# Weight splits pinned to the written order, and transposes of the compressed keys further behind their rotation

## The chip, the cores and the metric

The kernel runs on one core of one Trainium2 chip. The metric is the device time of one execution in microseconds (us), the median of several runs. The engines are named as the profile names them: PE multiplies matrices (PEld loads its weights), DVE is the vector engine, ACT the scalar engine, POOL the general one, SP the queue that issues the loads. Each engine has its own instruction stream and works through it in order; an instruction that waits for another engine holds up everything behind it on its own engine.

## The reference

Two layers, 256 positions, model width 1024, all in float32. What matters is the shape of the work:

```
for layer in range(2):
    h = rmsnorm(x, pre_norm[layer])
    proj = h @ w_in[layer]                  # 1024 x 7704, thirteen pieces
    hq, hf, hi, hz, nq, kc, vc, ks, vs, kw, vw, ng, nz = split(proj)
    o_h = rmsnorm(hgrn2(hq, hf, hi)) * silu(hz)            # gated linear recurrence, 8 heads
    k_cmp = rope(compress(kc));  v_cmp = compress(vc)      # 15 compressed blocks
    o_n = attention(rope(nq), (k_cmp, v_cmp), (rope(ks), vs), (rope(kw), vw), ng) * silu(nz)
    y = concatenate([o_h, o_n]) @ w_out[layer]
    x = x + rmsnorm(y, post_norm[layer])
```

## The kernel before

Every weight is used once for the 256 positions. To multiply at float32 accuracy, a weight and an activation are each cut in two float32r parts, and a product is three matmuls: high by high, and the two mixed ones. The weights of both layers are 168 **units** (`plan`, L182 to L192), numbered here from 0, of 128 partitions by 1024 (or 1072) elements, 84 to a layer. A unit goes through four steps. A load of 512 KB on SP's queue brings it into one of five `raw` buffers. ACT copies it to `whi`, rounded to the high part (L202). DVE subtracts that from `raw` and writes the rest to `wlo` (L203). Then PE uses both, in six to 24 matmuls; `whi` and `wlo` have eight buffers each.

The projections are written in the order nq, hf (here called the forget gates), kc/vc, kw, ks, hq, hi, hz, nz and then the output projection. PE's lines: L368 to L370 (`mm_a`: activations moving, 128x512 or narrower), L378 to L380 (`mm_b`: 128x256), L492/L493 (the compression), L997 to L999 (output projection). L351 transposes the normalised `h` of each half `a` of the positions, ACT's L355 and DVE's L356 make `Hhi` and `Hlo` of it, and these are what the next layer's first matmuls wait for.

What else DVE and ACT do beside the splits, as far as it is named below:
- The recurrence (`hgrn_fast`, L767 to L814): per layer two chains of some 25 DVE instructions, with two scans each (L769, L793) of the 128x1024 elements. The first chain works in the buffers `sA0` to `sA3`, the second in `sB0` to `sB3`.
- `kcvc` (L477 on ACT, L478 on DVE): splits the inputs of the compression into `sN0` and `sN1`; each second L477 is issued only after the first L478.
- `vals` and the gates: L560 (ACT), L561 (DVE), L587 (ACT).
- `compress`: `yp` is copied on ACT (L499), summed (L504, L506) and multiplied again (`second`); the keys are rotated (`rope`, L386 on ACT and L390 to L393 on DVE, into `kst`), transposed on PE (L531, in `third`) and split (`split_k`, L540 on ACT, L541 on DVE). The full keys take L552 for the transposes. L608 to L610 are the attention scores, which read them.
- `finish` (L1002): the end of a layer for one half `a`: L1008 and L1009, L331/L332 (root and reciprocal), L1014, then `norm_in`: L339, L344, and `turn_h` with L351.

Code is written in the order of a clock that the kernel keeps itself: each matmul advances `clock` by its ideal duration (`tick`), and `later(lag, fn, ch)` puts a function off by `lag` us of that clock. A unit's split is put off in this way by `LAG` = 9 us behind the point where its load is written, or until it is taken. That is the written order. The framework then orders each engine's stream at build time by its own estimates, so what runs may stand far from where it was written. `tc.keep_in_program_order` excludes an instruction from that: it is not issued before what was written ahead of it on its engine. Other instructions may still move.

Of the kernel before, what the change touches and what calls it, by code (L numbers as in the profile page):

```python
# [10 lines left out]
F32 = mybir.dt.float32  # L11
# [4 lines left out]
OP = mybir.AluOpType  # L16
# [25 lines left out]
CP = (2.0, 3.0)  # L42
L1 = (3.0, 3.0)
L2 = (5.0, 5.0)
L3 = 3.0
LQ = 4.0
LK = 8.0
LH = 10.0
# [47 lines left out]
def build(ctx, tc, A, out):  # L96
    nc = tc.nc
    V, S, P = nc.vector, nc.scalar, nc.tensor
# [23 lines left out]
    def later(lag, fn, ch):  # L122
        heapq.heappush(heap, (clock[0] + lag, count[0], ch, fn))
        count[0] += 1
# [69 lines left out]
    class Ring:  # L194
# [4 lines left out]
        def convert(self, n):  # L199
            while len(self.split) < n:  # L200
                raw, hi, lo, shaped = self.made[len(self.split)]
                S.copy(out=hi, in_=raw)  # L202
                V.tensor_tensor(out=lo, in0=raw, in1=hi.bitcast(F32), op=OP.subtract)  # L203
                self.split.append((shaped(hi), shaped(lo)))

        def fill(self, n=RING):
# [280 lines left out]
    def compress(l, i, ring, KC):  # L487
# [26 lines left out]
        def second():  # L514
# [19 lines left out]

            later(L3, third, "c0")

# [601 lines left out]
```

## Time and profile before

| what | value |
|---|---|
| median of 3 runs | 566.41 us (566.41 to 568.52) |
| the profiled execution | 566.25 us, its span 564.5 us |
| PE busy | 548.2 us (97% of the span) |
| PE's weight loads busy | 490.3 us (87%) |
| DVE busy | 398.0 us (71%) |
| ACT busy | 332.2 us (59%) |
| loads and stores | 96.55 MB, mean 171 GB/s |

The profile is one execution. The first two lines are times of the device; the span is the part of the execution in which engines work, and the 1.75 us beside it lie around it. Busy shares are averages over the span.

### The profile page before, as it was taken

The numbers are of one execution on the slowest core, as the hardware profiler recorded it, in microseconds if no ns is written. First come the engines' busy times: TensorE is split into PE (matmuls) and PEld (weight loads), VectorE is DVE, ScalarE is ACT, GpSimd is POOL, SyncE is SP. The second block draws the span as 40 slices with busy tenths as digits, with TensorE's granted clock in tenths as the row PEclk, the third lists the DMA queues.
The fourth block names the chain that finished last, engine by engine and source line by source line (L and its number), as shares of the span: only waits on it lengthen the run. The fifth ranks groups of instructions, "written<-read, shape, count | busy, mean of one in ns | idle before, by whom it ended". The sixth has DMA issues, their size and how long they took to land. (4 is left out here: it accounts for less than half of the span.)

```text
span 564.5 us, 9581 instructions
## 1 busy us (share of the span) xinstructions
PE 548.2 (97%) x3563; PEld 490.3 (87%) x3563; DVE 398.0 (71%) x880; ACT 332.2 (59%) x626; POOL 9.6 (2%) x18
## 2 busy tenths in 40 slices
PE   7999999999999999999989999999999999999993
PEld 4889998999888989988878999879988898998882
DVE  4897997889577277663678599878967654866422
ACT  6577447855366785552557763686626768746310
POOL 4000000000000001001000000000000000000000
PEclk9999999999999999999999999999999999999997
DMA  8697559953146058565475755698423622856111
GB/s 302 204 315 236 150 149 280 302 175 114 38 126 194 21 186 291 162 214 151 133 240 170 230 151 157 197 303 257 117 72 82 170 87 70 301 172 202 40 38 43
DMA packets 72196, 96.55 MB, mean 171 GB/s; under 512 B 3383, under 2 KB 49229, under 8 KB 72142
## 3 DMA queue, kind: packets, MB, share of 16 engines
q1 hardware_dynamic: 72142, 95.86, 55.3%
q8 instruction: 30, 0.49, 0.3%
q14 instruction: 24, 0.20, 0.1%
HBM read 93.75 MB, written 2.10 MB: 170 GB/s over the span
## 5 line engine op out<-in xcount | busy, mean ns | idle before, releaser
L203 DVE TENSOR_TENSOR wlo<-raw,whi 128x1024 fp32r<-128x1024 f32 (+1 forms) x168 | 202.8, 1222 | 60.4 <-ACT whi L202 57.4
L202 ACT CAST whi<-raw 128x1024 fp32r<-128x1024 f32 (+1 forms) x168 | 175.0, 1052 | 89.0 <-PE ps_mm L379 24.4
L378 PE MATMUL ps_mm<-Hhi,whi 128*128 128x256 f32 x448 | 127.5, 285 | 0.0
L379 PE MATMUL ps_mm<-Hlo,whi 128*128 128x256 f32 x448 | 125.7, 281 | 0.0
L380 PE MATMUL ps_mm<-Hhi,wlo 128*128 128x256 f32 x448 | 125.7, 280 | 0.0
L368 PE MATMUL ps_mm<-whi,Hhi 128*128 128x512 f32 (+1 forms) x256 | 101.5, 397 | 2.3 <-ACT Hhi L355 2.3
L369 PE MATMUL ps_mm<-wlo,Hhi 128*128 128x512 f32 (+1 forms) x256 | 98.9, 386 | 0.0
L370 PE MATMUL ps_mm<-whi,Hlo 128*128 128x512 f32 (+1 forms) x256 | 98.8, 387 | 0.0
L379 PEld LDWEIGHTS ps_mm<-Hlo,whi 128*128 128x128 f32 x448 | 84.5, 189 | 0.1
L378 PEld LDWEIGHTS ps_mm<-Hhi,whi 128*128 128x128 f32 x448 | 84.3, 188 | 0.1
L380 PEld LDWEIGHTS ps_mm<-Hhi,wlo 128*128 128x128 f32 x448 | 84.4, 188 | 0.0
L368 PEld LDWEIGHTS ps_mm<-whi,Hhi 128*128 128x128 f32 x256 | 48.9, 191 | 10.2 <-ACT Hhi L355 3.0
L370 PEld LDWEIGHTS ps_mm<-whi,Hlo 128*128 128x128 f32 x256 | 48.6, 190 | 10.2 <-DVE Hlo L356 0.3
L369 PEld LDWEIGHTS ps_mm<-wlo,Hhi 128*128 128x128 f32 x256 | 48.8, 191 | 7.6 <-DVE wlo L203 0.5
L627 DVE CUSTOM_DVE_ANT_0 ps_s<-ps_s,cm 128x128 f32<-128x128 f32 (+1 forms) x64 | 22.4, 370 | 2.1 <-PE ps_s L610 0.7
L630 ACT ACTIVATE sB<-ps_s,nm 128x256 f32<-128x256 f32 (+1 forms) x40 | 16.9, 430 | 10.8 <-DVE nm L627 10.1
L671 DVE TENSOR_TENSOR sB<-ps_t,sB 128x512 fp32r<-128x512 f32 x12 | 8.2, 687 | 20.1 <-ACT sB L670 20.1
L1009 DVE TENSOR_TENSOR sA<-ps_mm,sB 128x512 f32<-128x512 f32 x6 | 4.2, 692 | 21.6 <-ACT st L1008 21.6
L997 PE MATMUL ps_mm<-whi,sN 128*128 128x512 f32 x48 | 19.0, 396 | 0.0
L998 PE MATMUL ps_mm<-wlo,Hhi 128*128 128x512 f32 x48 | 19.0, 395 | 0.0
L999 PE MATMUL ps_mm<-whi,Hlo 128*128 128x512 f32 x48 | 18.9, 395 | 0.0
L999 PE MATMUL ps_mm<-whi,sN 128*128 128x512 f32 x48 | 18.9, 394 | 0.0
(282 smaller groups left out, 927.7 us busy)
## 6 DMA issues: line engine op xcount, KB each, us to landing
raw<-in_w_in SPq DMA_DIRECT2D x112, 512.0 KB, 4.6
raw<-in_w_out SPq DMA_DIRECT2D x32, 512.0 KB, 4.3
raw<-in_w_in SPq DMA_DIRECT2D x8, 536.0 KB, 4.7
raw<-in_cmp_w_k SPq DMA_DIRECT2D x16, 256.0 KB, 3.3
raw<-in_cmp_w_v SPq DMA_DIRECT2D x16, 256.0 KB, 3.3
sB<-in_x SPq DMA_DIRECT2D x3, 512.0 KB, 3.5
sB<-in_post_norm SPq DMA_DIRECT2D x2, 512.0 KB, 5.4
xs<-sB SPq DMA_DIRECT2D x4, 256.0 KB
```

The source lines that it names most:

```text
L202: S.copy(out=hi, in_=raw)
L203: V.tensor_tensor(out=lo, in0=raw, in1=hi.bitcast(F32), op=OP.subtract)
L368: P.matmul(out=ps, lhsT=hh, rhs=wh, start=k == 0, stop=False)
L369: P.matmul(out=ps, lhsT=hh, rhs=wl, start=False, stop=False)
L370: P.matmul(out=ps, lhsT=hl, rhs=wh, start=False, stop=k == KT - 1)
L378: P.matmul(out=ps, lhsT=wh, rhs=hh, start=k == 0, stop=False)
L379: P.matmul(out=ps, lhsT=wh, rhs=hl, start=False, stop=False)
L380: P.matmul(out=ps, lhsT=wl, rhs=hh, start=False, stop=k == KT - 1)
L627: V.tensor_tensor_reduce(out=sb[b], in0=sb[b], in1=mk[b], scale=-1.0, scalar=3e38, op0=OP.add, op1=OP.min, accum_out=nm[:, i, b:b + 1])
L997: P.matmul(out=ps, lhsT=hi, rhs=wh, start=first, stop=False)
L998: P.matmul(out=ps, lhsT=hi, rhs=wl, start=False, stop=False)
L999: P.matmul(out=ps, lhsT=lo, rhs=wh, start=False, stop=last)
```

## The change

Both instructions of a split, L202 on ACT and L203 on DVE, are pinned to the order in which they are written. And `L3`, the lag of `third` behind the rotation of the compressed keys, goes from 3 to 5 us of the kernel's own clock.

```diff
-L3 = 3.0
+L3 = 5.0
...
         def convert(self, n):
             while len(self.split) < n:
                 raw, hi, lo, shaped = self.made[len(self.split)]
-                S.copy(out=hi, in_=raw)
-                V.tensor_tensor(out=lo, in0=raw, in1=hi.bitcast(F32), op=OP.subtract)
+                tc.keep_in_program_order(S.copy(out=hi, in_=raw))
+                tc.keep_in_program_order(V.tensor_tensor(out=lo, in0=raw, in1=hi.bitcast(F32), op=OP.subtract))
                 self.split.append((shaped(hi), shaped(lo)))
```

The instructions are the same before and after; their order is not. Three places:

**DVE at the first layer's recurrence.** The number behind a name tells buffers apart; wlo_483, 509, 556, 574, 654, 673, 726 and 746 are the low parts of units 16 to 23. Before:

```order
71 L203 TENSOR_TENSOR wlo_509<-raw_507,whi_508 128x1024
72 L203 TENSOR_TENSOR wlo_556<-raw_554,whi_555 128x1024
73 L203 TENSOR_TENSOR wlo_574<-raw_572,whi_573 128x1024
...
99 L793 SCALAR_TENSOR_TENSOR sA3_441<-sA0_438,km_581,sN2_590 128x1023
100 L203 TENSOR_TENSOR wlo_673<-raw_671,whi_672 128x1072
101 L797 TENSOR_TENSOR sA2_440<-sA2_440,sA3_441 128x1024
102 L811 TENSOR_TENSOR sA0_438<-sA2_440,ce_579 128x512
103 L814 TENSOR_TENSOR sA0_438<-sA2_440,kx_589 128x512
104 L203 TENSOR_TENSOR wlo_726<-raw_724,whi_725 128x1072
105 L203 TENSOR_TENSOR wlo_746<-raw_744,whi_745 128x1072
106 L767 COPY fs_750<-sB0_592 128x32
```

With the change:

```order
94 L203 TENSOR_TENSOR wlo_483<-raw_481,whi_482 128x1024
95 L203 TENSOR_TENSOR wlo_509<-raw_507,whi_508 128x1024
96 L793 SCALAR_TENSOR_TENSOR sA3_441<-sA0_438,km_581,sN2_590 128x1023
97 L797 TENSOR_TENSOR sA2_440<-sA2_440,sA3_441 128x1024
98 L203 TENSOR_TENSOR wlo_556<-raw_554,whi_555 128x1024
99 L203 TENSOR_TENSOR wlo_574<-raw_572,whi_573 128x1024
100 L811 TENSOR_TENSOR sA0_438<-sA2_440,ce_579 128x512
101 L814 TENSOR_TENSOR sA0_438<-sA2_440,kx_589 128x512
102 L767 COPY fs_750<-sB0_592 128x32
103 L768 MEMSET sB0_592 128x32
104 L203 TENSOR_TENSOR wlo_654<-raw_652,whi_653 128x1072
```

The splits of units 16 to 19 stood ahead of the first chain of the recurrence and stand inside it now, and those of units 20 to 23 stood inside and ahead of the second chain and stand inside or behind it. wlo_726 and wlo_746 come after the second chain's L790.

**ACT at the compressed keys of the first layer.** Here kTh takes the high parts of the keys, whi_1200, 1212 and 1236 are units 36 to 38; ps_t_1287 before and ps_t_1340 after is the result of L531. Before, units 36 to 38 stand ahead of these rows:

```order
86 L202 CAST whi_1268<-raw_1267 128x1024
87 L202 CAST whi_1282<-raw_1281 128x1024
88 L386 ACTIVATE kst_1249<-ps_mm_1190 128x2x96
89 L540 CAST kTh_85<-ps_t_1287 128x2x15
90 L202 CAST whi_1301<-raw_1300 128x1024
91 L560 CAST vhi_90<-ps_mm_1190 128x256
92 L540 CAST kTh_85<-ps_t_1308 128x2x128
93 L499 COPY st_1323<-ps_s_1258 68x256
```

With the change:

```order
82 L386 ACTIVATE kst_1249<-ps_mm_1190 128x2x96
83 L540 CAST kTh_85<-ps_t_1303 128x2x128
84 L499 COPY st_1318<-ps_s_1258 68x256
85 L540 CAST kTh_85<-ps_t_1340 128x2x15
86 L560 CAST vhi_90<-ps_mm_1190 128x256
87 L202 CAST whi_1200<-raw_1199 128x1024
88 L202 CAST whi_1212<-raw_1211 128x1024
89 L202 CAST whi_1236<-raw_1235 128x1024
```

The copies of units 36 to 38 stood ahead of all of the keys' work and now stand behind it, behind L499 and L560 too. On PE, L531 stood in the middle of the compression's last matmuls, and now stands behind the last of them, followed at once by L608, L504 and L552, and these by unit 36.

**ACT at the boundary between the layers.** whi_3067, 3077, 3087, 3097 and 3107 are units 84 to 88, the first of the second layer; the L355 of ps_t_3125 and 3132 make `Hhi` for the first half of the positions, those of ps_t_3185 and 3192 for the second. Before:

```order
231 L202 CAST whi_3087<-raw_3086 128x1024
232 L339 ACTIVATE sA1_3050,ss_3051<-sB2_2823 128x512 x2
233 L202 CAST whi_3097<-raw_3096 128x1024
234 L202 CAST whi_3107<-raw_3106 128x1024
235 L331 ACTIVATE r1_3055<-ss_3051,eps_t_77 128x1
...
239 L355 CAST Hhi_87<-ps_t_3125 128x512
240 L355 CAST Hhi_87<-ps_t_3132 128x512
...
247 L355 CAST Hhi_87<-ps_t_3185 128x512
248 L355 CAST Hhi_87<-ps_t_3192 128x512
```

With the change:

```order
235 L202 CAST whi_3087<-raw_3086 128x1024
236 L1008 ACTIVATE st_3161,yss_3162<-ps_mm_2833 128x512
237 L1008 ACTIVATE st_3161,yss_3162<-ps_o_2834 128x512
238 L331 ACTIVATE r1_3168<-yss_3162,eps_t_77 128x1
239 L339 ACTIVATE sA3_3175,ss_3176<-sB3_2825 128x512 x2
240 L331 ACTIVATE r1_3180<-ss_3176,eps_t_77 128x1
241 L355 CAST Hhi_87<-ps_t_3185 128x512
242 L355 CAST Hhi_87<-ps_t_3192 128x512
243 L202 CAST whi_3097<-raw_3096 128x1024
244 L386 ACTIVATE st_3226<-ps_mm_3199 128x4x96
245 L202 CAST whi_3107<-raw_3106 128x1024
```

The copies of units 87 and 88 stood ahead of both halves' L355 and stand behind the second half's. On PE, the transposes of the first half (into ps_t_3125 and 3132) stood at the end of the first layer's last matmuls and now stand ahead of that layer's last nine; those of the second half stood among unit 90's matmuls, after units 84 to 89 of the first half, and now stand behind unit 86, before unit 87.

## Rows read from the trace of the kernel before

**Rows 1.** The page, busy times by engine, and the groups of the two split lines.

```profile
PE 548.2 (97%) x3563; PEld 490.3 (87%) x3563; DVE 398.0 (71%) x880; ACT 332.2 (59%) x626; POOL 9.6 (2%) x18
...
L203 DVE TENSOR_TENSOR wlo<-raw,whi 128x1024 fp32r<-128x1024 f32 (+1 forms) x168 | 202.8, 1222 | 60.4 <-ACT whi L202 57.4
L202 ACT CAST whi<-raw 128x1024 fp32r<-128x1024 f32 (+1 forms) x168 | 175.0, 1052 | 89.0 <-PE ps_mm L379 24.4
```

**Rows 2.** PE's waits: total us, times, longest (two of four rows).

```profile
PE ps_mm L368 <- ACT Hhi L355: 2.3, 2, 1.8
PE ps_t L531 <- DVE kst L393: 1.3, 1, 1.3
```

**Rows 3.** Busy time by stretch: length, PE, PEld, DVE, ACT, POOL; then clock, DMA.

```profile
51.00:85.00 34.00, 34.00 (x286) 34.00 (x285) 32.76 (x79) 15.66 (x24) 0.00 (x0) 1.00 0.54 156
...
325.00:359.00 34.00, 34.00 (x285) 33.90 (x285) 32.78 (x78) 18.22 (x28) 0.00 (x0) 1.00 0.49 143
```

**Rows 4.** Timeline of DVE at the recurrence: start, duration, line, operands.

```profile
51.53 0.18 DVE L767 COPY fs<-sA 128x32 f32<-128x32 f32 x1
...
62.65 0.68 DVE L814 TENSOR_TENSOR sA<-sA,kx 128x512 f32<-128x512 f32 x1
63.25 1.27 DVE L203 TENSOR_TENSOR wlo<-raw,whi 128x1072 fp32r<-128x1072 f32 x1
...
65.62 0.19 DVE L767 COPY fs<-sB 128x32 f32<-128x32 f32 x1
...
71.28 0.14 DVE L790 COPY sB<-km 128x1 f32<-128x1 f32 x1
```

**Rows 5.** Timeline of PE: first use of the low parts of units 22 and 28.

```profile
73.45 0.28 PE L369 MATMUL ps_mm<-wlo,Hhi 128*128 128x256 f32 x1
...
87.94 0.39 PE L369 MATMUL ps_mm<-wlo,Hhi 128*128 128x512 f32 x1
```

**Rows 6.** Timeline of ACT, 73 to 83 us, with the idle time before.

```profile
73.15 0.64 ACT L477 CAST sN<-ps_mm 128x256 fp32r<-128x256 f32 x1 [5.24 <-DVE sN L478]
...
82.66 0.19 ACT L587 ACTIVATE gt<-ps_s 128x24 f32<-128x24 f32 x1 [2.31 <-DVE vlo L561]
```

**Rows 7.** Timeline at the compressed keys, PE and then ACT.

```profile
102.28 0.28 PE L493 MATMUL ps_s<-wlo,sN 128*68 128x256 f32 x1
102.65 0.26 PE L531 MATMUL ps_t<-ct,kst 15*128 15x15 f32 x2
...
107.08 0.38 ACT L499 COPY st<-ps_s 68x256 f32<-68x256 f32 x1
```

**Rows 8.** Timeline at the boundary of the layers: PE, DVE, ACT.

```profile
284.68 0.50 PE L368 MATMUL ps_mm<-whi,Hhi 128*128 128x512 f32 x1 [1.80 <-ACT Hhi L355]
...
298.67 0.40 PE L368 MATMUL ps_mm<-whi,Hhi 128*128 128x512 f32 x1
...
288.99 1.41 DVE L1014 SCALAR_TENSOR_TENSOR sB<-sA,r,sB 128x512 f32<-128x512 f32 x2
...
291.96 1.41 DVE L344 SCALAR_TENSOR_TENSOR sA<-sB,r,sB 128x512 f32<-128x512 f32 x2
...
289.76 0.63 ACT L339 ACTIVATE sA<-sB 128x512 f32<-128x512 f32 x1 [2.70 <-DVE sB L1014]
```

**Rows 9.** Timeline of ACT at the start of the first layer.

```profile
19.06 0.59 ACT L355 CAST Hhi<-ps_t 128x512 fp32r<-128x512 f32 x1 [0.30 <-PE ps_t L351]
```

**Rows 10.** Timeline of PE in its first matmuls.

```profile
14.99 0.59 PE L370 MATMUL ps_mm<-whi,Hlo 128*128 128x512 f32 x1
15.42 0.40 PE L368 MATMUL ps_mm<-whi,Hhi 128*128 128x512 f32 x1
15.65 0.40 PE L369 MATMUL ps_mm<-wlo,Hhi 128*128 128x512 f32 x1
```

**Rows 11.** Busy time by stretch behind PE's last matmul, columns as before.

```profile
557.00:558.00 1.00, 0.00 (x0) 0.00 (x0) 0.78 (x2) 0.16 (x1) 0.00 (x0) 1.00 0.00 0
558.00:559.00 1.00, 0.00 (x0) 0.00 (x0) 0.80 (x2) 0.00 (x0) 0.00 (x0) 0.57 0.03 10
```

## The prediction

> **What bounds the kernel now.** I read the busy times first. PE is busy 97% of the span, and the two split lines are large, 202.8 us on DVE and 175.0 us on ACT, on engines with room on average [rows 1]. PE's waits come next: after the start it waits 2.3 us in two pieces for `Hhi` at the boundary of the layers and 1.3 us once for the rotated compressed keys, and hardly elsewhere [rows 2]. So PE sets the end, and an edit that takes no work from PE can win no more than these few us. What it can lose has to be read by stretch. From 51 to 85 us, and again in the second layer from 325 to 359 us, DVE is busy 32.8 of 34 us [rows 3]: there it is as full as PE, while PE does not wait. It does not wait because the splits of those units are done before DVE is full.
>
> **The change part by part.** No instruction is added, so the price is in what the new order makes late. I count each place in PE's own time: a low part that ends after PE would use it holds PE, and every later deadline moves by as much.
>
> *Recurrence, both layers.* In the new order four splits (units 16 to 19) that were finished ahead of the first L767 follow it. I walk down DVE's new order with the durations of before. The first chain, L767 at 51.53 to the end of L814 at 63.33 [rows 4], is 11.8 us and held two splits of 1.25, so 9.3 without; with the four splits at 1.22 [rows 1] it ends at 65.7. Then the second chain up to L790, 65.62 to 71.42 with one split in it [rows 4], is 4.6 without; the splits of units 20 and 21 (2.5) and two L478, each about as long as an L477 (0.64 [rows 6]), now stand in it. Unit 22's subtraction, at 63.25 before [rows 4], begins at 74.0 and ends at 75.25. PE wants it at 73.45 [rows 5]: 1.8 late, and unit 23 adds 0.5 by the same count. ACT agrees on this: unit 22's copy now stands behind the second L477, which before waited 5.24 us for the first L478 [rows 6]. From unit 23's end at 76.4, L793, L797, L811, L814 (4.8) and two L478 (1.3) lead to 82.5, a rotation to 83.2, units 24 and 25 to 85.6 and L561 to 86.0. The copy of unit 26 stands behind L587, which waits for L561 [rows 6]: it ends at 87.3, the subtraction at 88.5. PE wants that two units' matmuls (1.9) ahead of unit 28's 87.94 [rows 5], plus the 2.3 lost: 0.2 late. A second rotation and the copy behind it bring unit 27 to 90.4, 1.0 late; the next L561 and L587 bring the copy of unit 28 to 92.1 and its low part to 93.3, against 87.94 plus the 3.5 lost so far: 1.9 late. That makes 5.4. L767 could start up to 0.6 earlier than at 51.53, since its place is now ahead of splits that it followed; I take 5.1 for a layer, 10.2 for both. The bounds in a layer: nothing, if DVE caught up in gaps that I don't see, and 9.1, the 2.3 of the first two units and three more that each take a copy and a subtraction one after the other (2.27 [rows 1]) with PE idle.
>
> *Compressed keys.* The wait for the rotation goes: 1.3 in the second layer, and 0.37 less the usual step of 0.12 in the first, where L531 starts 102.65 after a matmul at 102.28 [rows 7]. What comes late in its place: L608 needs both L540, and the second stands behind L499 (0.38 [rows 7]), which needs the last matmul of the compression. That is about 0.8 us of an idle PE; then L609 waits 0.35 for L541, and unit 36, now behind L560, costs 0.33 for its high and 0.6 for its low part. 2.1 lost, 1.3 and 0.3 won: +2.6 over both layers, between -1.6 (nothing late) and +5.
>
> *Boundary.* The first half's transposes come earlier, so the wait of 1.80 with its neighbour, 2.0 together, goes [rows 8]. PE then starts at 282.7 (284.68 less 2.0) and is through units 84 to 86, 18 matmuls at 0.23 [rows 10], by 286.8. There stand the transposes of the second half. Their operand is made by a chain that before ran L1014 at 288.99, L339 at 289.76 and L344 at 291.96 to 293.37 [rows 8]. Two splits that stood ahead of its L1014 (2.4) stand behind it now: I count L1014 from 286.7, L339 to 289.0, L344 from 289.7, its first half ready at 290.4. PE stands 3.6 us, where before units 87 to 89 filled this time. The copies of units 87 and 88 stand behind the second half's L355: the high part of 87 comes at 293.2, the low at 294.5, the high of 88, behind L386 of unit 87's result, at 297.3. Each holds PE again (1.7, 1.1, 1.6). Adding the matmuls between, PE comes to the second use of unit 85 at 304.5, which before was at 298.67 [rows 8]: +5.8, the 2.0 won already inside. Bounds: -2.0, if the chain were in time, and 8.0, if nothing of the 2.0 were won.
>
> *The two small places.* At the start, the copy of unit 4 now stands behind the L355 that ended at 19.65 [rows 9], so it ends at 20.7, less 0.3 because the transposes come earlier; PE wants it as soon as the transposes are done that this L355 waited for, 19.0 or a little earlier: +1.4. Its bounds are 0 and 2.3, a copy and a subtraction. In the projections hi and hz the copies of units 56 to 59 stand behind L691 and other copies of PE's results; PE has other work in between, and I take +0.8 in a layer, 0 to 2.3: 1.6 for both.
>
> The other units I put at nothing: no unit waited before [rows 2], and through the attention PE has its scores and values between two units, so that a delay of a few us there reaches nobody; if that cover were gone, a copy and a subtraction (2.27) would be the price of one. Later splits also free the `raw` buffers and with them SP's loads later; a load has five units of time, so I put that at nothing too; it would cost where units go by fast, and there DVE is the later of the two anyhow.
>
> Sum: 10.2 + 2.6 + 5.8 + 1.4 + 1.6 = 21.6 us on the profiled 566.25 us, which is 0.16 below the median: **587.9 us**, 3.8% slower.
>
> Here the Trainium skill speaks against me. Its page "Perfetto Trace Analysis", section "Identifying the Most-Contended Engine", takes occupancy for DVE and the weight loads' busy share for PE: 87% against 71% [rows 1], so that delays on DVE should matter little, and the time would be that of the first rival. Its section "Optimization Strategy" adds that the most-contended engine can change between regimes, and with that the trace agrees [rows 3].
>
> **The rivals.** *The splits stay hidden.* Unit 22's low part was done at 64.5 [rows 4] and wanted at 73.45 [rows 5], 8.9 us early; if the new order still leaves them in time, only L531's waits go: 566.25 - 1.6 = 564.7 us, inside the 0.5% (2.8 us) that a measurement of this kernel can tell from no change. Against it stands the order itself: the same DVE work, in stretches with 1.2 us free of 34 [rows 3].
> *The boundary is won.* The first half's transposes come ahead of the last nine matmuls, and if the second half's operand is there when unit 86 is done (286.8), PE loses nothing: 564.7 - 2.0 = 562.7 us, faster by 0.65%. It is decided by whether L344 ends before 287; before it ended at 293.37 [rows 8], and only 2.4 us of splits leave its way. This also needs the recurrence hidden.
> *Half of it.* DVE catches up in one of the layers or the boundary's chain is shorter than counted, so that either a recurrence and a half (7.7) or the boundary's 5.8 drops out: 580 to 582 us; with both out, 574.
> *The array slows.* Between 286.8 and 294.5 PE would stand three times with little work between. Behind PE's last matmul the granted clock reads 1.00 at 557 to 558 us and 0.57 in the next row [rows 11], on its way to the lower of the two levels, 1.2 GHz, with PE idle since 555.3. If it falls at the boundary too, the matmuls behind go as at the start, every 0.43 us instead of every 0.23 [rows 10]; nine at that rate cost 1.8 and twelve 2.5: 590 us. At the old boundary, after 1.8 us of standing, the clock read 1.00. The Trainium skill's page "TensorE: Matmul & The Clock Gate", section "HAM oscillation — how this bites in real kernels", states that waits between bursts of matmuls send the clock down each time; by it this rival would be the likelier one.
>
> **How the numbers follow.** The forecast as summed 0.48; with the slower array 0.19; half of it 0.24; hidden 0.05; boundary won 0.04. The predicted time is the first's. The range holds the first three with their bounds, from 573 (both large terms cut) to 598 us (the slower array and the upper bounds of a third of the terms). Chances: faster by over 0.5% 0.04, within 0.06, slower 0.90.
>
> **What would show it.** PE's waits should list L369 or L380 for DVE's `wlo` near 75 and 90 us and again near 350 and 365, 4 to 6 us a layer, L351 for L344 of 3 to 4 us at the boundary, and L608 for `kTh`; the wait of L531 should be gone. DVE should be busy without a gap from 51 to 93 us. I am wrong if PE's row by stretch still reads 40 of 40 from 40 to 120 us, if L351 at the boundary doesn't wait, or if the time is lost where I count nothing, in the attention or behind 470 us.

## The result, and the profile after

The changed kernel takes 590.75 us (median of four runs, 589.87 to 592.32) against 566.41: a ratio of 1.0417, interval 1.0383 to 1.0451. The forecast of 587.9 us was 2.9 us low; the range held it. The profiled execution took 592.32 us, its span 590.4; it is the slowest of the four, so the account below, which follows it, adds up to more (26.06 us) than the 24.3 us between the medians.

The page of the changed kernel: busy time by engine, the granted clock in 40 slices, and the two split lines, which answer to [rows 1].

```profile
PE 561.2 (95%) x3563; PEld 497.8 (84%) x3563; DVE 400.3 (68%) x880; ACT 327.4 (55%) x626; POOL 9.6 (2%) x18
...
PEclk9999998999999999999969999899999999999998
...
L203 DVE TENSOR_TENSOR wlo<-raw,whi 128x1024 fp32r<-128x1024 f32 (+1 forms) x168 | 200.0, 1223 | 48.2 <-ACT whi L202 47.0
L202 ACT CAST whi<-raw 128x1024 fp32r<-128x1024 f32 (+1 forms) x168 | 169.6, 1051 | 20.0 <-PE ps_o L999 11.4
```

The splits cost what they cost: 1223 and 1051 ns each. The same 3563 matmuls, however, take 13 us longer, and the clock's row has three dips that the kernel before had not: part of the loss is a slower array. The rest is waiting. PE's waits in the changed kernel (total us, times, longest), beside [rows 2]:

```profile
PE ps_mm L368 <- ACT whi L202: 5.5, 5, 1.6
PE ps_mm L369 <- DVE wlo L203: 4.4, 5, 2.0
PE ps_t L351 <- DVE sA L344: 4.3, 2, 3.4
...
PE ps_s L608 <- ACT kTh L540: 1.2, 2, 0.6
PE ps_mm L380 <- DVE wlo L203: 0.8, 2, 0.4
PE ps_mm L368 <- ACT Hhi L355: 0.8, 1, 0.8
```

L531's wait is gone, as the prediction said, and splits that nothing waited for before now hold PE for 10.7 us (5.5, 4.4 and 0.8).

**Where the time goes.** I followed PE's lateness: for each unit, the start of the last matmul that uses its high part, after minus before. Unit 167, the last one, is used last at 554.86 us before and at 580.92 after, 26.06 later. Differences between such points give each stretch its share; the prediction's terms stand beside them, and the last column is the experiment *fill the wait*, explained below.

| stretch (units) | predicted | the change | fill the wait |
|---|---|---|---|
| start (to 3) | 1.4 | 1.66 | 1.15 |
| recurrence, first layer (3 to 31) | 5.1 | 5.52 | 3.99 |
| compressed keys, first layer (31 to 43) | 1.8 | 1.34 | 1.34 |
| rest of the first layer (43 to 81) | 0.8 | 0.89 | 0.92 |
| boundary (81 to 91) | 5.8 | 9.75 | 7.76 |
| recurrence, second layer (91 to 115) | 5.1 | 5.80 | 4.77 |
| compressed keys, second layer (115 to 127) | 0.8 | 0.18 | 0.17 |
| rest (127 to 167) | 0.8 | 0.92 | 0.92 |
| sum | 21.6 | 26.06 | 21.02 |

The boundary is counted from unit 81, ahead of the first half's transposes: four of these moved ahead of unit 83's last matmul, which adds 0.5 us to the lateness there without any wait. The stretches with the clock's dips are the recurrences and the boundary. Busy time by stretch in the changed kernel: length, then PE, PEld, DVE, ACT and POOL, clock, DMA.

```profile
51.00:85.00 34.00, 32.85 (x273) 32.44 (x272) 33.43 (x76) 15.94 (x23) 0.00 (x0) 1.00 0.58 174
...
85.00:93.00 8.00, 6.96 (x53) 6.14 (x52) 5.91 (x12) 4.80 (x9) 0.00 (x0) 1.00 0.74 219
...
94.00:97.00 3.00, 3.00 (x9) 2.35 (x8) 2.82 (x3) 1.26 (x3) 0.00 (x0) 0.50 0.81 237
...
298.00:300.00 2.00, 0.17 (x1) 0.20 (x2) 1.39 (x4) 0.48 (x3) 0.00 (x0) 0.64 0.56 213
300.00:306.00 6.00, 3.92 (x12) 2.81 (x12) 2.96 (x4) 2.11 (x3) 0.00 (x0) 0.50 0.05 6
306.00:312.00 6.00, 4.49 (x13) 3.10 (x13) 4.20 (x7) 4.75 (x6) 0.00 (x0) 0.50 0.40 108
...
367.00:373.00 6.00, 5.41 (x24) 5.42 (x25) 6.00 (x6) 1.47 (x3) 0.00 (x0) 0.50 0.59 172
```

From 51 to 85 us, the first row, PE is no longer busy throughout (32.85 of 34 us, against 34.00 in [rows 3]), while DVE went from 32.76 to 33.43: the engine that was full has become the one that is waited for. Rows with 0.50 are the lower of the clock's two levels, 1.2 GHz. At 94 to 97 us PE is busy for all 3.00 us, and yet only nine matmuls begin. In the timeline of PE, the waits stand in brackets at the end of a row:

```profile
76.22 0.39 PE L369 MATMUL ps_mm<-wlo,Hhi 128*128 128x256 f32 x1 [0.94 <-DVE wlo L203]
77.41 0.39 PE L369 MATMUL ps_mm<-wlo,Hhi 128*128 128x256 f32 x1 [0.21 <-DVE wlo L203]
...
92.21 0.49 PE L368 MATMUL ps_mm<-whi,Hhi 128*128 128x512 f32 x1 [0.45 <-ACT whi L202]
93.47 0.58 PE L369 MATMUL ps_mm<-wlo,Hhi 128*128 128x512 f32 x1 [0.77 <-DVE wlo L203]
...
114.86 0.39 PE L380 MATMUL ps_mm<-Hhi,wlo 128*128 128x256 f32 x1 [0.38 <-DVE wlo L203]
...
299.83 1.94 PE L351 MATMUL ps_t<-ct,sA 128*128 128x128 f32 x8 [3.38 <-DVE sA L344]
303.40 0.80 PE L368 MATMUL ps_mm<-whi,Hhi 128*128 128x512 f32 x1 [1.62 <-ACT whi L202]
304.66 0.80 PE L369 MATMUL ps_mm<-wlo,Hhi 128*128 128x512 f32 x1 [0.46 <-DVE wlo L203]
305.25 0.63 PE L370 MATMUL ps_mm<-whi,Hlo 128*128 128x512 f32 x1
...
308.67 0.79 PE L368 MATMUL ps_mm<-whi,Hhi 128*128 128x512 f32 x1 [1.51 <-ACT whi L202]
...
367.59 0.58 PE L369 MATMUL ps_mm<-wlo,Hhi 128*128 128x256 f32 x1 [1.98 <-DVE wlo L203]
```

At the boundary PE stands 3.38 us for the second half's operand and then three times for splits, 6.97 us in all against 2.0 before [rows 8]. A matmul of 128x512 takes 0.80 us there behind a wait and 0.63 in a row, where before it took 0.50 and 0.40 [rows 8].

### The profile page after: what moved, and what is told of

It is laid out like the page before. It is cut to its first block, busy times and chain, and to the rows that moved or that the text cites. A ratio compares the mean times of both kernels' runs of the same rounds, so it can differ in the third digit from the quotient of the medians.

```text
span 590.4 us, 9499 instructions
## 1 busy us (share of the span) xinstructions
PE 561.2 (95%) x3563; PEld 497.8 (84%) x3563; DVE 400.3 (68%) x880; ACT 327.4 (55%) x626; POOL 9.6 (2%) x18
## 5 line engine op out<-in xcount | busy, mean ns | idle before, releaser
L203 DVE TENSOR_TENSOR wlo<-raw,whi 128x1024 fp32r<-128x1024 f32 (+1 forms) x168 | 200.0, 1223 | 48.2 <-ACT whi L202 47.0
L202 ACT CAST whi<-raw 128x1024 fp32r<-128x1024 f32 (+1 forms) x168 | 169.6, 1051 | 20.0 <-PE ps_o L999 11.4
L380 PE MATMUL ps_mm<-Hhi,wlo 128*128 128x256 f32 x448 | 125.9, 281 | 0.8 <-DVE wlo L203 0.8
L368 PE MATMUL ps_mm<-whi,Hhi 128*128 128x512 f32 (+1 forms) x256 | 104.6, 409 | 6.3 <-ACT whi L202 5.5
L369 PE MATMUL ps_mm<-wlo,Hhi 128*128 128x512 f32 (+1 forms) x256 | 101.8, 398 | 4.4 <-DVE wlo L203 4.4
L370 PE MATMUL ps_mm<-whi,Hlo 128*128 128x512 f32 (+1 forms) x256 | 100.5, 393 | 0.0
L380 PEld LDWEIGHTS ps_mm<-Hhi,wlo 128*128 128x128 f32 x448 | 84.4, 188 | 1.2 <-DVE wlo L203 1.2
L368 PEld LDWEIGHTS ps_mm<-whi,Hhi 128*128 128x128 f32 x256 | 50.2, 196 | 17.3 <-ACT whi L202 8.7
L369 PEld LDWEIGHTS ps_mm<-wlo,Hhi 128*128 128x128 f32 x256 | 50.3, 196 | 13.9 <-DVE wlo L203 6.3
L370 PEld LDWEIGHTS ps_mm<-whi,Hlo 128*128 128x128 f32 x256 | 50.1, 196 | 10.0 <-DVE Hlo L356 0.3
L390 DVE TENSOR_TENSOR rt<-ps_mm,ct 128x128 f32<-128x128 f32 (+1 forms) x16 | 4.1, 255 | 24.7 <-ACT st L386 13.3
L998 PE MATMUL ps_mm<-wlo,sN 128*128 128x512 f32 x48 | 18.9, 394 | 0.0
```

The source lines that it names most:

```text
L202: tc.keep_in_program_order(S.copy(out=hi, in_=raw))
L203: tc.keep_in_program_order(V.tensor_tensor(out=lo, in0=raw, in1=hi.bitcast(F32), op=OP.subtract))
L368: P.matmul(out=ps, lhsT=hh, rhs=wh, start=k == 0, stop=False)
L369: P.matmul(out=ps, lhsT=hh, rhs=wl, start=False, stop=False)
L370: P.matmul(out=ps, lhsT=hl, rhs=wh, start=False, stop=k == KT - 1)
L380: P.matmul(out=ps, lhsT=wl, rhs=hh, start=False, stop=k == KT - 1)
```

## The experiments

Eleven kernels ran. In the first batch the change is taken apart; in the second one place or the distance is changed; the third tests the clock and looks for a better order. The table gives each kernel's time, its ratio to the kernel before with the interval, and the mean granted clock of its profiled execution (0.994 for the kernel before, 0.975 for the change).

| kernel | us | ratio | clock |
|---|---|---|---|
| L3 alone | 570.03 | 1.0045 (1.0023 to 1.0066) | 0.992 |
| pins alone | 590.29 | 1.0397 (1.0361 to 1.0433) | 0.980 |
| only ACT's copies pinned | 590.14 | 1.0403 (1.0368 to 1.0438) | 0.985 |
| only DVE's subtractions pinned | 592.76 | 1.0452 (1.0415 to 1.0489) | 0.986 |
| boundary free | 581.15 | 1.0278 (1.0249 to 1.0307) | 0.992 |
| recurrences free | 586.94 | 1.0386 (1.0355 to 1.0418) | 0.982 |
| LAG 4 | 574.50 | 1.0149 (1.0120 to 1.0178) | 0.988 |
| LAG 1 | 568.15 | 1.0040 (1.0026 to 1.0054) | 0.996 |
| fill the wait | 586.21 | 1.0336 (1.0315 to 1.0357) | 0.993 |
| boundary pinned alone, LAG 1 | 564.73 | 0.9962 (0.9948 to 0.9977) | 0.994 |
| pinned from unit 8, LAG 1 | 567.07 | 1.0004 (0.9987 to 1.0021) | 0.992 |

### The change taken apart

*L3 alone.*

```diff
-L3 = 3.0
+L3 = 5.0
```

> Only L3 goes from 3 to 5; no split is pinned. My theory (the pins cost, the lag wins): PE's wait of L531 for the rotated keys is gone and nothing else is late, so the time falls by the 1.4 us of the second layer and 0.3 of the first, to about 564.7 us, -0.3%. Rival (the longer lag is what costs, because the scores then wait for the keys' split): L608 waits for L540 in both layers, 1 to 3 us in all, and the time is 567 us or more.

570.03 us, so the gain did not come. That time is in the rival's range, but the rival's wait, L608 for L540, is not there either. PE's waits in this kernel:

```profile
PE ps_mm L368 <- ACT Hhi L355: 2.7, 1, 2.7
...
PE ps_t L504 <- ACT st L499: 2.1, 2, 1.9
```

L531's wait did go; PE's lateness falls by 1.7 us at unit 119. But the next step of the same chain then waits: the transposes L504 stand for ACT's copy L499, 2.1 us in two pieces, and unit 127 has 2.6 back. A small wait was moved down its own chain. The other 2.2 us lie at the boundary, which the edit does not reach: the copy of unit 90 waited there 3.05 us for its load, against 2.19 in the kernel before, with L1008 and L355 behind it on ACT; PE stood 2.66 us in place of 1.80, and the clock fell.

```profile
284.00:286.00 2.00, 0.55 (x1) 0.50 (x2) 1.05 (x2) 2.00 (x6) 0.00 (x0) 0.75 1.08 356
286.00:288.00 2.00, 2.00 (x6) 1.57 (x5) 2.00 (x5) 1.70 (x4) 0.00 (x0) 0.50 0.44 155
```

Six matmuls begin in 2 us where nine would at the high clock. Why that load came later in this execution is open.

*Pins alone, and each pin alone.*

```diff
-                S.copy(out=hi, in_=raw)
-                V.tensor_tensor(out=lo, in0=raw, in1=hi.bitcast(F32), op=OP.subtract)
+                tc.keep_in_program_order(S.copy(out=hi, in_=raw))
+                tc.keep_in_program_order(V.tensor_tensor(out=lo, in0=raw, in1=hi.bitcast(F32), op=OP.subtract))
```

> Both instructions of a split pinned, L3 left at 3. My theory: the whole loss is the pins', so 588 to 594 us, with the same three stretches of PE's clock at half and the wait of L531 back where the order allows it. Rival (the two parts of the change collide, and neither costs much alone): below 575 us.

> Only the copies (ACT, L202) pinned, the subtractions free, L3 at 3. My theory: a subtraction cannot run before its copy, so with the copies late most of the loss stays, above all at the boundary of the layers, where unit 87's copy stands behind the second half's L355: 580 to 592 us. Rival (the loss is DVE's, the full engine from 51 to 93 us, and only pinned subtractions bring it): 566 to 572 us.

> Only the subtractions (DVE, L203) pinned, the copies free, L3 at 3. My theory: the subtractions stand late in DVE's order whatever ACT does, so the recurrence still loses its 3 to 6 us a layer and the boundary part of its 9.7: 576 to 590 us. Rival (the copies' place is what holds the units, since ACT's copies wait for PE's results): 566 to 572 us.

The pins alone cost 1.0397, which the interval does not tell from the whole change: `L3` adds nothing that these runs can tell. (Of the three falls of the clock that I expected there, two came; over 94 to 97 us it read 1.00.) And either pin by itself costs as much as both. A split is a chain of two steps, and one late step is enough: a subtraction cannot start before its copy, and an early copy is no use while its subtraction is kept back. With only the subtractions pinned, PE's waits are fewer and longer:

```profile
PE ps_mm L369 <- DVE wlo L203: 9.3, 4, 3.5
PE ps_t L351 <- DVE sA L344: 5.2, 2, 4.1
PE ps_s L608 <- ACT sN L630: 2.9, 4, 1.3
```

PE waits there 9.3 us for low parts and hardly for a high part; with only the copies pinned it is 6.1 for low and 5.1 for high parts.

### Which place, and which order

*Boundary free, recurrences free.* The change, but units 82 to 91, or units 14 to 35 and 98 to 119, are left unpinned.

```diff
+                keep = tc.keep_in_program_order if not 82 <= len(self.split) < 92 else (lambda i: i)
+                keep(S.copy(out=hi, in_=raw))
+                keep(V.tensor_tensor(out=lo, in0=raw, in1=hi.bitcast(F32), op=OP.subtract))
```

> The change, but units 82 to 91 (the ones around the boundary of the layers) are not pinned; the order elsewhere is the change's. My theory (each late place costs by itself): the 9.7 us that PE falls behind at the boundary go, the old wait of 2 us included in that, and PE's clock has no slow stretch there: 581 us, 579 to 583. Rival (lateness made up later: a unit that is not late at the boundary only waits at the next place, since DVE is behind anyway): 586 us or more.

> The change, but units 14 to 35 and 98 to 119 (those of the recurrence and the compression, both layers) are not pinned. My theory: the 5.5 and 5.75 us lost there go, with the slow clock behind 93 and 367 us: 579.5 us, 577 to 582. Rival (DVE is simply full there, and the work only moves): 586 us or more.

Freeing ten splits at the boundary won 9.6 us of medians, as expected: PE's lateness grows by 0.21 us there, not 9.75, and waits elsewhere stay. Freeing 44 in the recurrences won only 3.8, and my expectation of 579.5 missed. (The kernel before was 0.9 us faster beside these two than beside the change. By the ratios the gains are 7.9 and 1.8 us, and the second is not clear of the change's interval.) In the first layer it worked: units 3 to 31 lose 0.97 us in place of 5.52. In the second it did not. The splits' waits are gone, but two others came (lines stand one higher in this kernel):

```profile
PE ps_s L493 <- ACT gt L588: 1.8, 2, 1.2
PE ps_t L505 <- ACT st L500: 1.5, 1, 1.5
```

and the clock reads 0.72 over 380 to 386 us. So units 91 to 115 lose 4.76 us there; the boundary still loses 9.9. Freeing a stretch inside a pinned row doesn't give back the order of before; I take it that what is pinned on either side shifts what is free, which no run shows by itself.

*The distance.* The change, with the distance between a unit's load and its split cut from 9 us to 4 and to 1.

```diff
-LAG = 9.0
+LAG = 1.0
```

> The change with LAG 4 instead of 9, so that a unit's split is written, and pinned, 5 us earlier of the kernel's own clock. My theory (the place at which a split is pinned is what costs, and two to three units stand earlier now at each of the late places): half of the loss is back, 574 to 582 us. Rival (a pinned split that waits for its load blocks DVE and ACT, so that an earlier place is worse): 590 us or more.

> The change with LAG 1. At the recurrence and at the boundary three to five units more stand ahead of the chains that they were behind. My theory: nearly all of the loss is back, 566 to 572 us, with the start's 1.7 us left, since the first eight units are not affected by LAG. Rival (early splits hold the chains of the recurrence and of finish instead, or wait for loads): 575 us or more.

Both came out as expected: 574.50 and 568.15 us. So it isn't pinning as such that costs: the written order asked for the splits too late. With a distance of 1 us the recurrences' waits for splits are gone, and the boundary does better than before: the lateness falls from 1.98 us at unit 81 to 0.34 at unit 91, 1.64 won. (The expectations below say 2.16. That counts from unit 83 and includes the 0.5 us of transposes that only moved.)

### The clock, and a better order

*Fill the wait.* The change, with 34 idle transposes on PE at the boundary: 24 ahead of the second half's transposes and 10 behind them. The order of the rows on ACT, DVE and SP is unchanged. In this kernel L351 holds the idle transposes, L353 and L362 the real and the ten further ones, and L374 to L376 stand for L368 to L370.

```diff
+                for k in range(fill * (1 - q)):
+                    P.transpose(out=ps[:, 0:128], in_=xa[:, 0:128], identity=ident)
...
+            if fill:
+                ps = tb()
+                for k in range(10):
+                    P.transpose(out=ps[:, 0:128], in_=h[:, 0:128], identity=ident)
```

> The change, with 34 transposes of 128x128 added to TensorE's row at the layer boundary: 24 ahead of the eight transposes of the second half's input, which waited there 3.4 us for VectorE's line 344, and 10 behind them, where the next matmul waited 1.6 us for a weight copy. They write banks that are overwritten or never read; the rows of ScalarE, VectorE and the queues stay as they were. The before-last batch and the profile of the change left open what the slow clock there costs (0.50 from 300 to 312 us, matmuls of 128x512 every .427 us in place of .233) and what brings it. Theory, the array's idleness brings the clock down and the slow clock is a loss of its own: with the two waits filled the granted clock stays at 1.00 over 296 to 312 us, the matmuls there stay at .23 us, and about 3.6 us of the boundary's 9.7 come back, 586 to 588 us. Rival, the clock falls for another reason, or the waits that lie behind it set the time anyway: the clock is at 0.50 there again or the boundary's loss stays at 9 us or more, 590 to 594 us.

586.21 us, inside the theory's 586 to 588, though not by the way that I wrote: at the boundary 2.0 us came back, not 3.6, and the clock did not stay at 1.00 to the end. Busy time by stretch, the same stretches as above:

```profile
298.00:300.00 2.00, 1.22 (x10) 0.78 (x9) 1.26 (x3) 1.42 (x3) 0.00 (x0) 1.00 0.00 0
300.00:306.00 6.00, 3.83 (x20) 2.77 (x20) 3.62 (x7) 3.23 (x5) 0.00 (x0) 0.87 0.30 89
306.00:312.00 6.00, 6.00 (x25) 4.90 (x24) 4.17 (x5) 2.22 (x3) 0.00 (x0) 0.84 0.79 223
...
367.00:373.00 6.00, 6.00 (x51) 6.00 (x50) 6.00 (x12) 3.11 (x7) 0.00 (x0) 1.00 0.29 89
...
94.00:97.00 3.00, 3.00 (x15) 2.43 (x14) 2.76 (x4) 1.68 (x3) 0.00 (x0) 1.00 0.95 265
```

and PE's timeline at the boundary:

```profile
294.87 2.81 PE L351 MATMUL ps_t<-ct,sB 128*128 128x128 f32 x24 [0.42 <-issue]
297.75 1.38 PE L353 MATMUL ps_t<-ct,sA 128*128 128x128 f32 x8
...
302.35 0.40 PE L376 MATMUL ps_mm<-whi,Hlo 128*128 128x512 f32 x1
...
304.95 0.79 PE L374 MATMUL ps_mm<-whi,Hhi 128*128 128x512 f32 x1 [1.51 <-ACT whi L202]
...
379.75 0.50 PE L375 MATMUL ps_mm<-wlo,Hhi 128*128 128x512 f32 x1 [0.76 <-DVE wlo L203]
```

While the wait was filled, the clock stayed at 1.00: the transposes cost 0.117 us each (2.81 for 24), and the matmuls behind them 0.40. It fell in the longest wait that was left unfilled, 1.51 us, behind shorter ones of 0.65 and 0.68, and rose again by about 308. The boundary lost 7.76 us in place of 9.75, so the work that nobody uses won 2.0 us. In the change eight transposes took 1.94 us there, four more and twelve matmuls of 128x512 also went at the low rate; at 0.1 and 0.19 us more each I estimate 3.5 us, of which five matmuls and four transposes, 1.4, are still slow here. That agrees. The other part of the gain I had not foreseen: at 94 and at 367 us, where neither kernel's rows differ from the other's, the clock fell in the change's profiled execution and did not in this one. 15 matmuls begin in 94 to 97 us, against nine. *Pins alone* (the first row) and *boundary free* (the second) also have the change's rows on PE, ACT and DVE up to 97 us, and the clock stayed up at 94 us in both:

```profile
94.00:97.00 3.00, 3.00 (x16) 2.41 (x15) 2.98 (x3) 1.70 (x4) 0.00 (x0) 1.00 0.76 215
...
94.00:97.00 3.00, 3.00 (x15) 2.42 (x14) 2.85 (x4) 1.68 (x4) 0.00 (x0) 1.00 0.88 251
```

The fall at 94 us came in one of four executions with the same rows. It goes with that execution, which took 1.57 us more than the median, rather than with the change. Between the two profiles the slow clock in the recurrences is worth 1.5 and 1.0 us (5.52 less 3.99, 5.80 less 4.77). In the second layer the difference is 2.2 us up to unit 111, but then this kernel waits 0.76 us for a low part at 379.75 us, for which the change, later by then, has no wait.

*Boundary pinned alone, LAG 1.* The kernel before, with only units 82 to 91 pinned and the distance at 1 us.

```diff
-LAG = 9.0
+LAG = 1.0
...
+                keep = tc.keep_in_program_order if 82 <= len(self.split) < 92 else (lambda i: i)
```

> The kernel before, with only the splits of units 82 to 91 pinned and the distance between making a unit's raw buffer and splitting it cut from 9 to 1 us (at that distance the pinned row has units 84 to 88 behind the norm of the layer boundary and ahead of its transposes' copies). Theory, a pinned row gains where its written order puts the splits off until the norm is done: the 1.96 us wait of line 368 at the boundary goes, as in the change with the distance of 1 us (2.16 won there), and without that version's losses at the start (1.54) and in the recurrence: 563.5 to 565 us. Rival, the copies pushed behind the norm are late for their matmuls, or the gain is given back at the next wait of the recurrence: 566 to 568 us.

564.73 us, a ratio of 0.9962 (0.9948 to 0.9977): faster than the kernel before, by little, but the interval excludes no change, and the best of all. PE's row gained 1.63 us from unit 81 to unit 91, like the 1.64 of the change with LAG 1, and kept it to the end. ACT's timeline shows how (its L203 is the copy L202, L356 is L355):

```profile
274.35 0.29 ACT L332 ACTIVATE r<-ss,eps_t 128x1 f32<-128x1 f32 x1 [0.23 <-DVE ss L342]
274.55 4.83 ACT L203 CAST whi<-raw 128x1024 fp32r<-128x1024 f32 x5
279.39 1.07 ACT L356 CAST Hhi<-ps_t 128x512 fp32r<-128x512 f32 x2
280.88 1.05 ACT L203 CAST whi<-raw 128x1024 fp32r<-128x1024 f32 x1 [0.41 <-DMA raw<-in_w_in]
```

In the kernel before, ACT at the same place:

```profile
282.52 1.04 ACT L202 CAST whi<-raw 128x1024 fp32r<-128x1024 f32 x1 [2.19 <-DMA raw<-in_w_in]
...
284.05 1.07 ACT L355 CAST Hhi<-ps_t 128x512 fp32r<-128x512 f32 x2
```

Before, the L355 that PE waited for stood on ACT behind a copy whose load had not landed: those 2.0 us of waiting were a late transfer, passed on through ACT's order. In this kernel the two L355 stand ahead of that copy, unit 90's, and of the one shown, unit 89's; and on PE the first half's transposes stand ahead of the layer's last nine matmuls, as in the change. A kernel with LAG 1 and no pin was not run, so how much of this the shorter distance would do alone is not shown.

*Pinned from unit 8, LAG 1.*

```diff
-LAG = 9.0
+LAG = 1.0
...
+                keep = tc.keep_in_program_order if len(self.split) >= 8 else (lambda i: i)
```

> The kernel before, with all splits from unit 8 on pinned and the distance at 1 us; the compressed keys' transposes at 3 as before. Against the change with the distance of 1 us (568.15) this leaves the start free (1.54 lost there) and gives back the longer wait of the keys. Theory, the written order is harmless wherever it is near the order that the scheduler chose, and gains 2.16 at the boundary: 565 to 567 us. Rival, the recurrence with its splits pinned costs 2 us or more in each layer at any distance: 569 us or more.

567.07 us, just above the upper end of the expectation: no different from the kernel before. The start is free of its loss (PE's lateness is -0.07 us at unit 3) and the boundary wins 1.64. In the second layer it is lost again in the profiled execution (568.64 us, where seven of the twelve took 565.18 to 567.09): L504 (here L505) waits 2.4 us for L499 (here L500) in two pieces over both layers, the clock reads 0.66 over 366 to 371 us, and units 107 to 113 lose 4.0.

## Why the prediction came out as it did

**The mechanism was right.** The splits moved behind work that they used to precede, DVE and ACT became what PE waits for, and PE lost at each of the places named. Most signs came as named: L369 waits for `wlo` near 76 and 93 us and again at 367 (L380 only later, at 115), L351 for L344 with 3.4 us, L608 for `kTh`, and nothing for L531. But the waits for splits in a recurrence add up to 2.7 and 2.6 us, where I wrote 4 to 6 a layer; what each stop costs beside the wait itself and, in this execution, the slow clock make up the rest of the lateness. DVE was to be busy without a gap from 51 to 93 us; it was until 85 (33.43 of 34), and from there to 93 only 5.91 of 8, because ACT's copies, behind L587, were the later ones.

**The term that was wrong is the clock.** I valued it at nothing and left it to a rival with a chance of 0.19 and a cost of 1.8 to 2.5 us at one place. In the profiled execution it fell at three places and cost about 3.5, 1.5 and 1.0 us, 6.0 in sum. The first is an estimate, of which *fill the wait* won back 2.0; the other two are differences between two single executions. The rival's mechanism was right, at 590 us; its cost for the boundary was low, and it named no other place.

**The waits were a little overcounted.** In the recurrences the loss with the clock up was 3.99 and 4.77 us a layer, against 5.1. Unit 22's subtraction began at 74.91 us with PE 1.66 late; counted so, mine was to begin at 75.7. DVE's chain ran 0.8 us ahead of my walk, and PE waited 0.94 there in place of 1.8. At the boundary I counted stops of 3.6, 1.7, 1.1 and 1.6 us; they were 3.38, 1.62, 0.46 and 1.51. The start (1.66 for 1.4; 1.15 in *fill the wait*, with the same rows) was within a few tenths. The keys cost 1.5 us over both layers in place of 2.6, and the two rests of a layer 1.8 in place of 1.6.

So two errors of opposite sign stood against each other: some 2 us too much waiting and 6 too little clock make most of the 4.5 us between 21.6 and 26.06. Against the 24.3 us between the medians, in which, to judge by the four executions above, the fall at 94 us is mostly missing, the miss is 2.7. That the forecast came so near is in part luck, since the errors offset each other. With the clock mostly kept up, as in *fill the wait*, the lateness is 21.02 us. The lower end of the range, 573, is also a little under what its words give: both large terms out make 574 in the paragraph on the rivals.

**The rivals.** *Hidden* fell with the first row of waits. Its part that concerns `L3` alone fell as well, on its own: 570.03 us where it gave 564.7. *The boundary won* did not come at a distance of 9 us; at 1 us the boundary won 1.64 us. *Half of it* did not happen.

By the Trainium skill's page "TensorE: Matmul & The Clock Gate", section "HAM oscillation — how this bites in real kernels", the long waits for loads between short bursts of matmuls in its example send the clock down each time. At the boundary the runs agree (behind 3.38 us of waiting: 0.50; with that wait filled: 1.00). Behind shorter waits it went both ways: behind 0.94 and 0.21 us at 76 and 77 us the clock stayed at 1.00, and behind the waits at 92 and 93 us, in identical rows, it fell in one execution and not in three others. The Trainium skill's page "Perfetto Trace Analysis", section "Identifying the Most-Contended Engine", calls the engine with the highest occupancy the most contended. By that DVE, at 71%, was not it, and I had read from this that its delays matter little; DVE's share fell from 71% to 68% and the kernel became 4.2% slower. The measurement decides: the share of the span was no guide here.

## What to carry to other kernels

Before you pin instructions to a written order, price each deadline on the engine that sets the end, stretch by stretch: a helper that is 71% busy over the span was 96% busy where it counted. Pin few, and where a row shows that something urgent stands behind a late transfer: here ten units at a short distance gained 0.4%, all 168 at that distance (with `L3` at 5) lost 0.4%, and all 168 at a long one lost 4.2%. When you add up waits on the matrix engine, add the slow clock behind them, and when you remove one, look a step further down its chain.

## What was unexpected

The slow clock outlasts the wait that precedes it: from 367 to 373 us PE is busy 5.41 of 6 us and the clock reads 0.50 throughout. How much standing brings it down is not settled by these runs: 1.80 us at the old boundary left it at 1.00, 1.51 us in *fill the wait*, behind earlier short waits, brought it down, as did 2.66 us with `L3` alone. And rows of identical order kept it in three executions and lost it in a fourth. Filling a wait with matrix work whose result nobody reads paid 2.0 us at the boundary, by faster matmuls behind it.
